# Layer 1's gate product: three 256-column matmuls a step in place of 512 and 256 columns, with no copy and addition of two halves

## Chip, cores, metric

The kernel runs on one core of a Trainium2 chip. The metric is device time in microseconds of one execution; the time before is the median of 3 runs. The core's engines are named as in the profile: PE (TensorE's matmuls), PEld (its weight loads), DVE (VectorE), ACT (ScalarE), POOL (GpSimd) and SP (SyncE, which here issues DMA transfers). SBUF is the core's working memory, and PSUM the eight accumulation banks into which PE writes.

## What is computed

Two layers of a diffusion transformer on 256 tokens of width 2048 and 256 context tokens, in fp32. Layer 0 mixes with a Fourier transform, layer 1 with attention. Only layer 1 matters here: 64 query heads of 64 channels, 8 key and value heads, a window of 128 tokens beside the context, and a sink in the softmax. Its result is multiplied by a gate, silu(z), before the output product:

```python
q, k, v, z = jnp.split(h @ w_in, [D_BRANCH, D_BRANCH + kvw, D_BRANCH + 2 * kvw], axis=-1)
...
y = jnp.moveaxis(o, 0, 1).reshape(b, n, D_BRANCH) * jax.nn.silu(z)
...
x = x + gate * (y @ w_out[i])
```

The change touches the product that makes z: 256 tokens by 2048, times 2048 by 4096.

## The kernel before

**Two parts for each number.** Products of full precision are made of a high part, which PE reads as fp32r, and a low part, the remainder. `split` makes them: ACT casts the high part (line 66), DVE subtracts it to get the low part (line 67). For a weight W = wh + wl and an activation h = hi + lo, the product is wh·hi + wh·lo + wl·hi. The helper `mm3` (lines 145 to 147) issues these as three matmuls into one PSUM region. The activations of layer 1 lie in 16 tiles `hx1[k]` of 128 x 512, one for each 128 input channels: columns 0 to 255 are the high parts of the 256 tokens, columns 256 to 511 the low parts. Both parts are therefore side by side.

**A gate block** is 128 of the 4096 gate channels, and there are 32. A block takes 16 steps, one for each `k`, in two units of 8 steps. Each step has the weights as the stationary operand (128 x 128, wh or wl) and the activations as the moving one. Before, wh meets all 512 columns of `hx1[k]` in one matmul (line 1451), so that wh·hi comes to stand in columns 0 to 255 of the PSUM bank and wh·lo in columns 256 to 511; wl meets the 256 high columns in a second matmul (line 1453), added to columns 0 to 255. In the last step the order of the two is turned round. Then ACT copies the second half out of PSUM into a tile `zs` (line 1457), DVE adds the first half to it (line 1458), ACT takes the tanh of half of that (line 1459), and DVE makes (tanh + 1)·z (line 1460), which is twice silu(z). The product with the attention's output is line 1472.

**Around it.** The blocks are fillers for PE in the attention of layer 1. A loop over 64 heads `i` puts down the scores of head `i` (`stage_s`), a unit of other work, the values of head `i - 2` (`stage_o`), and another unit. The units come from a list: the query product of a group of 8 heads (8 units), then that group's 4 gate blocks (2 units each), and at the end the first part of the output product.

- `stage_s`: scores on PE (lines 1489 and 1490), mask and maximum on DVE (line 1491), exponential on ACT (line 1494), normalised probabilities f as a high part on ACT (line 1506) and a low part on DVE (line 1507), then a DMA transpose `ft<-f` (line 1509).
- `stage_o`: values times transposed probabilities on PE (lines 1524 and 1525), out through ACT (line 1530) and DVE (line 1531).
- Queries: out of PSUM on ACT (line 1357), rotated on POOL (lines 1132 to 1138), transposed on PE (line 1370) and split (lines 1373 to 1376).
- Weights: loaded by SP 1 MB at a time into three buffers `raw` (line 50), split in halves, one unit ahead of use.

The order on each engine isn't the order of the code: a scheduler sets it when the program is built, by its own estimate of when each instruction could run. An engine runs its instructions in that order, and waits at the head of its list.

Of the kernel before, what the change touches and what calls it, by code (L numbers as in the profile page):

```python
# [10 lines left out]
F32 = mybir.dt.float32  # L11
# [3 lines left out]
ALU = mybir.AluOpType  # L15
AX = mybir.AxisListType

P = 128
D = 2048
KT = D // P  # L20
DB = 4096
NB = DB // P
N = 256
# [9 lines left out]
def tile_dit(ctx: ExitStack, tc: tile.TileContext, a: dict, out: bass.AP):  # L33
    nc = tc.nc
    V, S, PE, GP = nc.vector, nc.scalar, nc.tensor, nc.gpsimd
# [8 lines left out]
    def psum():  # L44
        return pp.tile([P, 512], F32, tag="ps", name="ps")
# [98 lines left out]
    def mm3(o, wh, wl, xh, xl, start, stop):  # L144
        PE.matmul(o, wh, xh, start=start, stop=False)  # L145
        PE.matmul(o, wh, xl, start=False, stop=False)  # L146
        return PE.matmul(o, wl, xh, start=False, stop=stop).ins  # L147
# [711 lines left out]
    with tc.tile_pool(name="yp", reuse_waits="tile", bufs=32) as ypool:  # L859
# [39 lines left out]
        if True:  # L899
# [21 lines left out]
            for kg in range(4):  # L921
# [10 lines left out]
                for j in range(4):  # L932
                    k = kg * 4 + j
                    wh, wl = w[j // 2]
                    for b in range(4):
                        q = slice((j % 2) * 512 + b * P, (j % 2) * 512 + (b + 1) * P)
# [7 lines left out]
            for b in range(4, NB):  # L944
# [9 lines left out]
                o = psum()  # L954
                for k in range(KT):
# [13 lines left out]
                    wh, wl = w[k // 8]  # L969
                    q = slice((k % 8) * P, (k % 8 + 1) * P)  # L970
# [60 lines left out]
        for i in range(32):  # L1031
            sw, kg = i // 16, i % 16
            if kg == 0:
                o = [psum() for _ in range(8)]
# [9 lines left out]
            if kg == 14:  # L1044
                q = gt0[:, sw * 8 : sw * 8 + 8].rearrange("p k s -> p (k s)")
# [21 lines left out]
            for j, b in [(j, b) for b in range(8) for j in range(2)] if edge else [(j, b) for j in range(2) for b in range(8)]:  # L1067
                q = slice(b * P, (b + 1) * P)
# [35 lines left out]
    with tc.issue_after(st_end[0]):  # L1104
        o = psum()
# [34 lines left out]
    with tc.tile_pool(name="h1", reuse_waits="tile", bufs=16) as h1p:  # L1140
        hx1 = []
# [3 lines left out]
        with tc.tile_pool(name="kvp", reuse_waits="tile", bufs=2) as kvp:  # L1145
# [4 lines left out]
            for k in range(KT):  # L1150
                z2 = kvp.tile([P, 1024], F16, tag="hz", name="hz", bufs=16)
                t = kvp.tile([P, 512], F32, tag="ht", name="ht")
                for s in range(2):
                    q = slice(s * N, (s + 1) * N)
# [40 lines left out]
            o = [[psum() for _ in range(2)] for _ in range(4)]  # L1195
            for kg in range(8):
# [16 lines left out]
                for j in range(2):  # L1213
                    k = kg * 2 + j
                    wh, wl = w[j]
                    for tb in range(4):
                        c = tb // 2 * 512 + tb % 2 * P
                        for kv in range(2):
                            q = slice(kv * 512, (kv + 1) * 512)
# [40 lines left out]
        with tc.tile_pool(name="at", reuse_waits="tile", bufs=2) as at:  # L1260
# [55 lines left out]
            def o1_step(k, os_, wh, wl):  # L1316
                while len(yh) <= min(k + 4, NB - 1) and (len(yh) < 28 or fin):
                    y_split(len(yh))
                for tb in range(2):
                    mm3(os_[tb], yh[k][:, tb * P : (tb + 1) * P], yh[k][:, N + tb * P : N + (tb + 1) * P], wh, wl, k == 0, k == NB - 1)  # L1320
# [17 lines left out]
            def prep_kk(hk):  # L1338
                kkh = at.tile([P, 512], F32R, tag="kkh", name="kkh")
                kkl = at.tile([P, 512], F32R, tag="kkl", name="kkl")  # L1340
                b = (hk % 2) * 64
                src = kT[hk // 2][b : b + 64, :]
                for c in (0, 64):
                    S.copy(kkh[c : c + 64, :], src)
                for c in (0, 64):
                    GP.tensor_tensor(kkl[c : c + 64, :], src, kkh[b : b + 64, :].bitcast(F32), op=ALU.subtract)
                kk[hk] = (kkh, kkl)

            def finish_q(hk, oq):
                qr = []  # L1350
                for tb in range(2):
                    t = act()
                    if hk == 0:
                        roped(t, oq[tb], tb, actp, "act")
                    else:
                        t0 = act()
                        S.copy(t0, oq[tb])
                        roped(t, t0, tb, actp, "act", GP)
                    qr.append(t)
                if hk:  # L1360
                    prep_kk(hk)
                for p2 in range(2):
                    defer.append((slot[0], lambda p2=p2: q_turn(hk, p2, qr)))
# [38 lines left out]
            def prep(u):  # L1402
                kind, n, i, _ = u
                if kind == "o":
                    return w1_next()
                src = (kind, n, i // 2)
                if src not in raws1:
                    raws1[src] = raw(a["wq"][n, i // 2] if kind == "q" else a["wz1"][n])
                return half_split(raws1[src], i % 2)
# [3 lines left out]
            def emit_unit():  # L1413
                if pos[0] >= len(ulist):
                    return
                u = ulist[pos[0]]
                if pos[0] not in ready:
                    ready[pos[0]] = prep(u)
                if pos[0] + 1 < len(ulist):
                    ready[pos[0] + 1] = prep(ulist[pos[0] + 1])  # L1420
                w = ready.pop(pos[0])
                pos[0] += 1
                kind, n, i, o = u
                if kind == "o":
                    if n == 0:
                        oA.extend([psum(), psum()])
                    for j in range(2):
                        o1_step(n * 2 + j, oA, *(t[:, j * 512 : (j + 1) * 512] for t in w))
                    return
                wh, wl = w  # L1430
                if kind == "q":
                    if i == 0:
                        o += [psum(), psum()]
                    if (n, i) == (0, 4):
                        with tc.issue_after(last_cast[0]):
                            prep_kk(0)
                    for j in range(2):
                        k = i * 2 + j
                        q = slice(j * 512, (j + 1) * 512)
                        for tb in range(2):  # L1440
                            mm3(o[tb], hx1[k][:, tb * P : (tb + 1) * P], hx1[k][:, N + tb * P : N + (tb + 1) * P], wh[:, q], wl[:, q], k == 0, k == KT - 1)
                    if i == 7:
                        finish_q(n, o)
                else:
                    if i == 0:
                        o.append(psum())
                    for k in range(i * 8, i * 8 + 8):
                        q = slice((k % 8) * P, (k % 8 + 1) * P)
                        for part in (0, 1) if k < KT - 1 else (1, 0):
                            if part == 0:  # L1450
                                PE.matmul(o[0], wh[:, q], hx1[k], start=k == 0, stop=k == KT - 1)  # L1451
                            else:
                                PE.matmul(o[0][:, 0:N], wl[:, q], hx1[k][:, 0:N], start=False, stop=False)  # L1453
                    if i == 1:
                        th = at.tile([P, N], F32, tag="th", name="th", bufs=3)
                        zs = at.tile([P, N], F32, tag="zs", name="zs", bufs=1)
                        S.copy(zs, o[0][:, N : 2 * N])
                        V.tensor_tensor(zs, o[0][:, 0:N], zs, op=ALU.add)
                        S.activation(th, zs, AF.Tanh, scale=0.5)
                        V.scalar_tensor_tensor(th, th, 1.0, zs, op0=ALU.add, op1=ALU.mult)  # L1460
                        szs[n] = th
                        emit_y(n)
# [3 lines left out]
            def emit_y(blk):  # L1466
                if blk not in szs or (blk, 1) not in obs or blk in ydone:
                    return
                ydone.add(blk)
                if blk % 2 == 0:  # L1470
                    y1.append(act())
                V.scalar_tensor_tensor(y1[blk // 2][:, (blk % 2) * N : (blk % 2 + 1) * N], obs[blk, 1], dsc[:, blk // 4 : blk // 4 + 1], szs.pop(blk), op0=ALU.mult, op1=ALU.mult)
                if blk % 2:
                    ypairs.append(slot[0] // 2)
# [62 lines left out]
            for i in range(first):  # L1537
                emit_unit()
                if i == 2:
                    for hp in range(4):  # L1540
                        k_turn(hp)
                if i == 5:
                    for half in range(2):
                        d_turn(half)
                if i >= 8 and defer:
                    defer.pop(0)[1]()

            def filler():
                j = slot[0]
                slot[0] += 1  # L1550
                emit_unit()
                if defer and defer[0][0] + 2 < j:
                    defer.pop(0)[1]()
# [23 lines left out]
        with tc.tile_pool(name="fin", reuse_waits="tile", bufs=1) as fp:  # L1577
# [41 lines left out]
            o = [[psum() for _ in range(2)] for _ in range(2)]  # L1619
            for kg in range(16):  # L1620
# [10 lines left out]
                for j in range(2):  # L1631
                    k = kg * 2 + j
                    wh, wl = w[j]
                    for tb in range(2):
                        for c in range(2):
                            q = slice(c * 512, (c + 1) * 512)
# [4 lines left out]
            o = [psum() for _ in range(2)]  # L1641
# [70 lines left out]
            for h in range(2):  # L1712
                q = slice(h * 256, h * 256 + 256)
# [107 lines left out]
```

## Time and profile before

| | before |
|---|---|
| median of 3 runs | 1764.61 us (1764.34 to 1765.5) |
| profiled execution | 1766.34 us |
| its span, first to last instruction | 1764.5 us |
| PE busy | 1728.8 us, 9539 matmuls |
| DVE busy | 1421.9 us |
| ACT busy | 1148.4 us |
| the gate blocks run from about | 1142 us to 1575 us |
| granted TensorE clock over the span | 0.998 |

The table's busy times are of one profiled execution; the median is of runs without a profile. A matmul's duration in the profile reaches from its start to the modelled end of its results, so consecutive matmuls overlap, and the pace of PE is read from the distance between starts. In a row such as `ps<-h,wh 128*128 128x512` the names are output, moving and stationary operand, then the size of the weights and that of the result.

### The profile page before, as it was taken

How to read it: one execution, taken by the hardware profiler on the slowest of the kernel's cores; microseconds unless marked ns; L12 is line 12 of the kernel's file. 1: busy time of each engine (PE TensorE's matmuls, PEld its weight loads, DVE VectorE, ACT ScalarE, POOL GpSimd, SP SyncE). 2: the span in 40 equal slices, each digit the busy share in tenths (PEclk: the TensorE clock that was granted, in tenths of full speed). 3: DMA queues.
4: the chain of work that ended last, by engine and by line, in shares of the span. 5: the costliest groups of instructions: out<-in, count | busy, mean ns of one | idle time of the engine just before them, and what ended most of it. 6: DMA issues, size and time to landing. Idle time of an engine off the chain costs nothing.

```text
span 1764.5 us, 26891 instructions
## 1 busy us (share of the span) xinstructions
PE 1728.8 (98%) x9539; PEld 1149.6 (65%) x9539; DVE 1421.9 (81%) x2475; ACT 1148.4 (65%) x2197; POOL 361.3 (20%) x485
## 2 busy tenths in 40 slices
PE   6999999999999999999999999999999999999998
PEld 4679999644444444446444745788888878877464
DVE  5769888798676787777698686899899889998755
ACT  5545556476777755465235596688888788897643
POOL 0002111211222105212311111412303221251001
PEclk9999999999999999999999999999999999999999
DMA  9998999778998869977996594688997897888643
GB/s 394 417 342 254 275 273 257 295 282 303 340 314 299 312 227 378 372 254 258 394 341 229 181 362 155 191 198 198 222 212 200 204 212 207 210 192 283 225 172 120
DMA packets 232296, 465.66 MB, mean 264 GB/s; under 512 B 154497, under 2 KB 154897, under 8 KB 205281
## 3 DMA queue, kind: packets, MB, share of 16 engines
q1 hardware_dynamic: 180672, 331.41, 58.5%
q0 software_dynamic: 47344, 125.58, 22.2%
q10 hardware_dynamic: 4144, 6.95, 1.2%
q8 instruction: 75, 1.23, 0.3%
q14 instruction: 61, 0.49, 0.1%
HBM read 419.30 MB, written 12.59 MB: 245 GB/s over the span
## 4 chain that ended last, share of the span: by engine, by line
PE 80%; DVE 8%; DMA 7%; ACT 3%; issue 2%; POOL 0%; POOLq 0%; ACTq 0%; DVEq 0%; SPq 0%
PE ps L145 23%; PE ps L146 23%; PE ps L147 22%; PE ps L1451 3%; DMA ft<-f 3%; DMA raw<-in_awp 2%; PE ps L1453 2%; DVE wl L67 2%; DVE f L1507 1%; PE ps L286 1%; DVE ps L1491 1%; PE ps L1489 1%; PE ps L1490 1%; PE ps L1524 1%; PE ps L1525 1%
## 5 line engine op out<-in xcount | busy, mean ns | idle before, releaser
L67 DVE TENSOR_TENSOR wl<-raw,wh 128x1024 fp32r<-128x1024 f32 x152 | 203.1, 1337 | 38.4 <-ACT wh L66 27.2
L146 PE MATMUL ps<-act,wf 128*128 128x512 f16 x512 | 194.0, 379 | 0.0
L147 PE MATMUL ps<-act,wf 128*128 128x512 f16 x512 | 191.1, 379 | 0.0
L145 PE MATMUL ps<-act,wf 128*128 128x512 f16 x512 | 189.8, 379 | 0.6 <-ACT wf L137 0.3
L66 ACT CAST wh<-raw 128x1024 fp32r<-128x1024 f32 x152 | 158.2, 1042 | 48.0 <-PE ps L146 29.1
L1451 PE MATMUL ps<-h,wh 128*128 128x512 f32 x512 | 184.8, 397 | 0.0
L145 PE MATMUL ps<-y,wf 128*128 128x512 f16 x448 | 169.8, 379 | 0.8 <-ACT wf L137 0.8
L146 PE MATMUL ps<-y,wf 128*128 128x512 f16 x448 | 169.8, 379 | 0.0
L147 PEld LDWEIGHTS <-wf 128*128 128x128 f16 x960 | 93.9, 98 | 113.3
L145 PEld LDWEIGHTS <-wf 128*128 128x128 f16 x960 | 93.7, 98 | 113.2 <-ACT wf L137 4.2
L147 PE MATMUL ps<-y,wf 128*128 128x512 f16 x448 | 164.9, 379 | 0.0
L146 PEld LDWEIGHTS <-wf 128*128 128x128 f16 x960 | 93.9, 98 | 109.0
L137 ACT ACTIVATE wf<-raw,nrm 128x1024 f16<-128x1024 f32 x56 | 63.5, 1145 | 130.1 <-PE ps L147 78.6
L1453 PE MATMUL ps<-h,wl 128*128 128x256 f32 x512 | 138.7, 281 | 0.3 <-DVE wl L67 0.3
L138 DVE SCALAR_TENSOR_TENSOR wf<-raw,tn,wf 128x1024 f16<-128x1024 f32 x64 | 79.8, 1281 | 42.5 <-ACT wf L137 41.8
L1494 ACT ACTIVATE p<-ps,mx 128x512 f32<-128x512 f32 x128 | 88.1, 689 | 39.7 <-DVE mx L1491 36.6
L829 ACT ACTIVATE act<-act 128x512 f32<-128x512 f32 x178 | 109.4, 616 | 5.9 <-DMA act<-in_wo 4.5
L790 POOL DMA_DIRECT2D wa<-in_adw x64 | 34.2, 535 | 371.7 <-PE ps L147 144.9
L1507 DVE SCALAR_TENSOR_TENSOR f<-p,sm,f 128x512 f16<-128x512 f32 x128 | 103.5, 829 | 8.3 <-ACT f L1506 8.0
L1451 PEld LDWEIGHTS ps<-h,wh 128*128 128x128 f32 x512 | 96.2, 188 | 18.9
L1506 ACT ACTIVATE f<-p,sm 128x512 f16<-128x512 f32 x128 | 88.0, 717 | 31.1 <-DMA ft<-f 18.4
L146 PE MATMUL ps<-wl,h 128*128 128x512 f32 x256 | 101.8, 398 | 0.6 <-DVE wl L67 0.6
(430 smaller groups left out, 4863.6 us busy)
## 6 DMA issues: line engine op xcount, KB each, us to landing
raw<-in_wz SPq DMA_DIRECT2D x64, 1024.0 KB, 5.9
raw<-in_awp SPq DMA_DIRECT2D x32, 1024.0 KB, 12.7
zr<-in_adw SPq DMA_DIRECT2D x64, 512.0 KB, 7.0
wa<-in_adw POOLq DMA_DIRECT2D x64, 512.0 KB, 6.6
act<-in_wo POOLq DMA_DIRECT2D x128, 256.0 KB, 7.7
raw<-in_wo SPq DMA_DIRECT2D x32, 1024.0 KB, 8.2
raw<-in_wq SPq DMA_DIRECT2D x32, 1024.0 KB, 5.3
raw<-in_wu SPq DMA_DIRECT2D x32, 1016.0 KB, 6.7
```

Source lines behind the costliest of these rows:

```text
L66: last_cast[0] = S.copy(h, src).ins
L67: last_sub[0] = eng.tensor_tensor(l, src, h.bitcast(F32), op=ALU.subtract).ins
L138: last_sub[0] = V.scalar_tensor_tensor(w[:, 1], src, up, w[:, 0], op0=ALU.mult, op1=ALU.subtract).ins
L145: PE.matmul(o, wh, xh, start=start, stop=False)
L146: PE.matmul(o, wh, xl, start=False, stop=False)
L147: return PE.matmul(o, wl, xh, start=False, stop=stop).ins
L829: S.activation(t, t, AF.Square, accum_out=c)
L1451: PE.matmul(o[0], wh[:, q], hx1[k], start=k == 0, stop=k == KT - 1)
L1453: PE.matmul(o[0][:, 0:N], wl[:, q], hx1[k][:, 0:N], start=False, stop=False)
L1494: S.activation(pt[tb], so[tb], AF.Exp, bias=mx[:, tb : tb + 1], scale=-1.0, accum_out=sm[:, tb : tb + 1])
L1506: fa = S.activation(f[:, 0:512], pt[tb], AF.Copy, scale=sm[:, tb : tb + 1]).ins
L1507: f_last[:] = fa, V.scalar_tensor_tensor(f[:, 512:1024], pt[tb], sm[:, tb : tb + 1], f[:, 0:512], op0=ALU.mult, op1=ALU.subtract).ins
```

## The change

Every step of a gate block goes through `mm3` with the moving operand cut into its two halves: wh with the 256 high columns, wh with the 256 low columns, wl with the high columns, all three added into columns 0 to 255 of the bank. The sum is complete in PSUM when the last step ends. The copy and the addition go, the tile `zs` with them, and tanh and the last operation read the bank.

```diff
                     for k in range(i * 8, i * 8 + 8):
                         q = slice((k % 8) * P, (k % 8 + 1) * P)
-                        for part in (0, 1) if k < KT - 1 else (1, 0):
-                            if part == 0:
-                                PE.matmul(o[0], wh[:, q], hx1[k], start=k == 0, stop=k == KT - 1)
-                            else:
-                                PE.matmul(o[0][:, 0:N], wl[:, q], hx1[k][:, 0:N], start=False, stop=False)
+                        mm3(o[0][:, 0:N], wh[:, q], wl[:, q], hx1[k][:, 0:N], hx1[k][:, N : 2 * N], k == 0, k == KT - 1)
                     if i == 1:
                         th = at.tile([P, N], F32, tag="th", name="th", bufs=3)
-                        zs = at.tile([P, N], F32, tag="zs", name="zs", bufs=1)
-                        S.copy(zs, o[0][:, N : 2 * N])
-                        V.tensor_tensor(zs, o[0][:, 0:N], zs, op=ALU.add)
+                        zs = o[0][:, 0:N]
                         S.activation(th, zs, AF.Tanh, scale=0.5)
                         V.scalar_tensor_tensor(th, th, 1.0, zs, op0=ALU.add, op1=ALU.mult)
```

Six lines fewer stand in the file, so what was line 1459 and later has a number lower by 6 in the changed kernel: tanh is line 1453 there, the high part of f 1500, the first values matmul 1518. The new matmuls carry the helper's lines, 145 to 147.

On PE, the start of the first gate block, whose first two steps are shown; `h` with a number is the tile `hx1[k]`. Before:

```order
L1451 MATMUL ps<-h_10253,wh 128x512
L1453 MATMUL ps<-h_10253,wl 128x256
L1451 MATMUL ps<-h_10258,wh 128x512
L1453 MATMUL ps<-h_10258,wl 128x256
L1451 MATMUL ps<-h_10263,wh 128x512
```

After:

```order
L145 MATMUL ps<-h_10253,wh 128x256
L146 MATMUL ps<-h_10253,wh 128x256
L147 MATMUL ps<-h_10253,wl 128x256
L145 MATMUL ps<-h_10258,wh 128x256
L146 MATMUL ps<-h_10258,wh 128x256
L147 MATMUL ps<-h_10258,wl 128x256
```

A step has three matmuls, and two in a row have the weights wh.

On ACT, the instructions behind the copy of the second gate block; `qa` and `qb` are split queries, `p` the exponentials, `es` the sink's share, `th` the gate's tanh. Before:

```order
L1373 CAST qa<-ps 64x512
L1374 CAST qb<-ps 64x512
L1459 ACTIVATE th<-zs 128x256
L1494 ACTIVATE p,sm<-ps,mx 128x512
L1495 ACTIVATE es<-mx,sink 128x2
L1506 ACTIVATE f<-p,sm 128x512 x2
L66 CAST wh<-raw 128x1024
L1373 CAST qa<-ps 64x512
L1374 CAST qb<-ps 64x512
```

After, at the same place:

```order
L1373 CAST qa<-ps 64x512
L1374 CAST qb<-ps 64x512
L1488 ACTIVATE p,sm<-ps,mx 128x512
L1489 ACTIVATE es<-mx,sink 128x2
L66 CAST wh<-raw 128x1024
L1373 CAST qa<-ps 64x512
L1374 CAST qb<-ps 64x512
L1500 ACTIVATE f<-p,sm 128x512 x2
```

The tanh has left this place (it stands where the copy stood), and the two f have moved behind a weight cast and the second pair of query copies. There are such exchanges on ACT and DVE throughout the stretch, most of them by a place or two; SP's list of weight loads and transposes changes in its first part.

## The prediction

> **What bounds the kernel now.** I read the page first, then the busy time of the stretch that the change touches, then what PE waited for there, and last the matmuls of one gate block in order of time.
>
> ```profile
> span 1764.5 us, 26891 instructions
> PE 1728.8 (98%) x9539; PEld 1149.6 (65%) x9539; DVE 1421.9 (81%) x2475; ACT 1148.4 (65%) x2197; POOL 361.3 (20%) x485
> ```
>
> PE is busy 98% of the span, and PE and PEld have the same number of instructions, so each matmul brings a weight load of its own, also where two in a row use the same weights. The profiled execution took 1766.34 us, 1.84 us more than its span, and lies 1.7 us above the median of the runs, 1764.61 us. The differences worked out below are added to the median.
>
> ```profile
> core 0: us, PE busy (x) PEld busy (x) DVE busy (x) ACT busy (x) POOL busy (x), PEclk, DMA share, GB/s
> 1142.00:1575.00 433.00, 429.37 (x2366) 356.69 (x2365) 401.79 (x746) 358.98 (x724) 105.23 (x78) 1.00 0.87 208
> ```
>
> This is the stretch in which all 32 gate blocks run, woven into the attention. PE is busy 429.4 of 433.0 us at the full clock (1.00), but VectorE is at 401.8 / 433.0 = 93% and the DMA engines at 0.87. Three resources are close to their limit; PE is the first. What PE waited for, in the same stretch:
>
> ```profile
> PE ps L1524 <- DMA ft<-f: 2.1, 4, 1.2
> PE ps L146 <- DVE wl L67: 0.6, 2, 0.4
> PE ps L1370 <- POOL act L1138: 0.5, 1, 0.5
> PE ps L1453 <- DVE wl L67: 0.3, 1, 0.3
> ```
>
> In all 3.5 us, of which 0.9 us ended with VectorE's low weight half and 2.1 us with a DMA transpose of the probabilities. So the stage runs at PE's pace, and two things count: what a step costs on PE, and how much of these 3.5 us goes or is added.
>
> **PE's pace, the main term.** A step was one matmul of 512 columns (weights wh, line 1451) and one of 256 (weights wl, line 1453), 512 times. It becomes three of 256: wh on the high half, wh again on the low half, wl on the high half. The columns streamed are the same, 768; there is one matmul and one weight load more.
>
> ```profile
> L1451 PE MATMUL ps<-h,wh 128*128 128x512 f32 x512 | 184.8, 397 | 0.0
> L1453 PE MATMUL ps<-h,wl 128*128 128x256 f32 x512 | 138.7, 281 | 0.3 <-DVE wl L67 0.3
> L1453 PEld LDWEIGHTS ps<-h,wl 128*128 128x128 f32 x512 | 96.6, 189 | 3.5 <-DVE wl L67 0.7
> L1451 PEld LDWEIGHTS ps<-h,wh 128*128 128x128 f32 x512 | 96.2, 188 | 18.9
> ```
>
> These durations (397 and 281 ns, loads 188 and 189) overlap each other, so they can't be added; the price is the distance from one start to the next. In the second gate block, in order of time:
>
> ```profile
> 1150.05 0.40 PE L1451 MATMUL ps<-h,wh 128*128 128x512 f32 x1
> 1150.29 0.28 PE L1453 MATMUL ps<-h,wl 128*128 128x256 f32 x1
> 1150.40 0.39 PE L1451 MATMUL ps<-h,wh 128*128 128x512 f32 x1
> ...
> 1154.91 0.39 PE L1451 MATMUL ps<-h,wh 128*128 128x512 f32 x1
> 1155.14 0.40 PE L1453 MATMUL ps<-h,wl 128*128 128x256 f32 x2
> 1155.38 0.40 PE L1451 MATMUL ps<-h,wh 128*128 128x512 f32 x1
> ```
>
> From the first to the fifteenth wh matmul there are 14 steps in 1154.91 - 1150.05 = 4.86 us: 347.1 ns a step. The row with x2 is the block's end, where two 256-column matmuls with new weights each follow one another: together they last 0.40 us where one lasts 0.28, so the second began 0.12 us after the first; with the group's mean of 281 ns for one, about 118 ns. That is the pace which the new step would have, inside this very stage: 3 x 118 = 354 ns. The change costs 354 - 347.1 = 6.9 ns a step, 512 x 6.9 = 3.5 us.
>
> Two other stages bound the 118 ns, the nearest rows with three 256-column matmuls a step:
>
> ```profile
> 31.42 0.28 PE L146 MATMUL ps<-dl,xh 128*128 128x256 f32 x1
> ...
> 34.59 0.28 PE L147 MATMUL ps<-dh,xl 128*128 128x256 f32 x1
> 222.85 0.28 PE L145 MATMUL ps<-act,wmh 128*127 128x256 f32 x1
> ...
> 228.48 0.28 PE L147 MATMUL ps<-act,wml 128*127 128x256 f32 x1
> ```
>
> The first run is 28 matmul starts in 3.17 us, 113.2 ns each; the second 47 in 5.63 us, 119.8 ns each, with the same weights (wmh) twice in a row as the new step has them. By the first a step takes 339.6 ns and the change wins 512 x 7.5 = 3.8 us; by the second it takes 359.4 and costs 512 x 12.3 = 6.3 us. I take 118, because it was measured among the same tiles, in the same stage, and lies nearer to the second.
>
> Of this the Trainium skill has a rule (TensorE: Matmul & The Clock Gate, "Back-to-back issue gap"): a warm matmul starts N/2.4 + 2.5 ns after the one before. By it the old step is 215.8 + 109.2 = 325.0 ns, the new one 327.5, and the change costs an estimated 1.3 us instead of 3.5. The step of 347.1 ns in the trace is longer than that rule allows, so the rows decide.
>
> **What leaves ACT and DVE.** Behind each block the copy (line 1457) and the addition (line 1458) go; the tanh and the last operation now read the PSUM bank itself.
>
> ```profile
> L1472 DVE SCALAR_TENSOR_TENSOR act<-ob,dsc,th 128x256 f32<-128x256 f32 x28 | 13.9, 495 | 0.1
> L1460 DVE SCALAR_TENSOR_TENSOR th<-th,zs 128x256 f32<-128x256 f32 x31 | 13.5, 436 | 0.4
> L1459 ACT ACTIVATE th<-zs 128x256 f32<-128x256 f32 x31 | 12.9, 416 | 3.3 <-DVE zs L1458 3.2
> L1458 DVE TENSOR_TENSOR zs<-ps,zs 128x256 f32<-128x256 f32 x31 | 12.7, 411 | 0.0
> L1457 ACT COPY zs<-ps 128x256 f32<-128x256 f32 x32 | 11.9, 373 | 0.7
> ```
>
> That is 32 x 0.411 = 13.2 us of DVE and 32 x 0.373 = 11.9 us of ACT. The tanh out of PSUM isn't in the trace: between the copy out of PSUM, 373 ns, and its own 416. The last operation with one operand in PSUM lies between 411 ns (line 1458, the same mix) and 495 (line 1472); I take 411, so nearly no change. At most 32 x 0.059 = 1.9 us of DVE are given back. DVE goes from 93% to about (401.8 - 13.2) / 436.5 = 89%. None of it is PE's time: it is worth only what it takes from PE's 3.5 us of waits. The bank is released by the second operation behind the block, as before. I count half of the 0.9 us that ended with DVE, 0.45 us, since the addition was one of many operations that a late wl stood behind, and nothing of the rest.
>
> **Sum.** 3.5 - 0.45 = +3.05 us: 1764.61 + 3.05 = 1767.7 us; the profiled execution would come to 1769.4. That is 0.17%, just under 0.2% (3.5 us), which is about what a measurement of this kernel can tell from no change.
>
> **Rivals.**
>
> *The relief pays for the pace* (17%). If the lighter DVE and ACT let every f and wl come early, all 3.5 us of waits go and the sum is 3.5 - 3.5 = 0: 1764.6. For it: DVE at 93%. Against it: the longest wait is on the transpose's own DMA.
>
> *The new order makes PE wait for transposes* (20%), the rival that ends slower. The scheduler placed ACT's and DVE's instructions anew. Behind the second gate block the normalised probabilities f (line 1506) now stand behind one weight cast and two q copies:
>
> ```profile
> L66 ACT CAST wh<-raw 128x1024 fp32r<-128x1024 f32 x112 | 116.5, 1040 | 0.8 <-PE ps L1453 0.4 <-PE ps L1451 0.3
> L1374 ACT CAST qb<-ps 64x512 fp32r<-64x512 f32 x14 | 8.2, 583 | 0.2
> L1373 ACT CAST qa<-ps 64x512 fp32r<-64x512 f32 x14 | 8.0, 575 | 0.0
> ```
>
> So f may begin 1.04 + 0.58 + 0.58 = 2.2 us later there, its transpose with it. Transposes leave little room: their landing varies by more than that, and PE already waits for some.
>
> ```profile
> DMA to landing us min/median/max: 3.0/5.1/7.8
> 1502.57 0.28 PE L1524 MATMUL ps<-ft,v 128*128 128x256 f16 x1 [0.41 <-DMA ft<-f]
> ```
>
> It decides from the point at which a transpose lands after PE has finished the matmuls placed ahead of line 1524. Priced at the stage's waits doubled, 3.5 us more: 3.5 + 3.5 = +7.0, 1771.6. Against it: PE's own order between scores and values hardly moves, and the relief works the other way.
>
> *The short pace* (7%). If the new steps run at 113.2 ns a matmul, the sum is -3.8 - 0.45 = -4.25: 1760.4. Against it: all 256-column matmuls of this stage start at 118.
>
> *The added weight load isn't hidden* (1%). Then each step pays the load's 188 ns, 512 x 0.188 = 96 us: 1861. Against it stands the old step: its two loads alone last 377 ns, more than the 347.1 ns of the whole step, so loads do run beside matmuls. In the Trainium skill (the same page, "The mechanism" in Part 3) stands that a weight load overlaps a running matmul only where the row groups differ, and these weights fill all rows; by that rule the load would be exposed. The trace disagrees with it here.
>
> That the change doesn't do what it says can be excluded: PE's list holds three matmuls a step, and the copy and the addition are gone.
>
> **Chances.** The forecast keeps 55%: its own range is the pace at 117 to 119 ns (351 to 357 ns a step, +2.0 to +5.1) less 0 to 0.9 us of relief, so +1.1 to +5.1, 1765.7 to 1769.7, of which I put four parts in ten above 3.5 us. Slower by over 0.2%: 0.22 + 0.20 + 0.01 = 0.43. Faster: the short pace, 0.07, and 0.03 of the relief case, 0.10. Within 0.2%: 0.33 + 0.14 = 0.47. The range from 1763.0 to 1772.0 leaves out the short pace (7%), the exposed load (1%), 2% of the relief case and two fifths of the new waits (8%): 18%.
>
> **What would show it.** In the profile after, steps of line 145 to 147 at 354 ns from wh to wh show the main term right; 340 or 359 would show one of the bounds. The share of DVE in the stage should fall to about 89%. PE's waits in the stage, on DMA ft and on wl, should come to about 3 us: near 0 is the relief case, 6 or more the order's. Wrong altogether would be a span that moves by more than the steps and these waits together, or the copy and addition showing up as PE time.

## The result and the profile after

The changed kernel is faster: 1761.26 us against 1764.37 us in the median of 12 runs each, a ratio of 0.9979 with a 95% interval of 0.9972 to 0.9986. That is 3.1 us, 0.2%, where the prediction had 3 us more. The profiled execution took 1761.24 us. Its page and the stretch of the gate blocks:

```profile
span 1759.3 us, 27829 instructions
PE 1726.3 (98%) x10051; PEld 1173.5 (67%) x10051; DVE 1404.7 (80%) x2443; ACT 1141.0 (65%) x2165; POOL 355.5 (20%) x485
1142.00:1575.00 433.00, 431.66 (x2888) 383.60 (x2887) 389.01 (x722) 356.63 (x702) 105.35 (x83) 1.00 0.84 207
```

PE has 512 matmuls and 512 weight loads more, DVE and ACT 32 instructions fewer each. DVE's busy share of the stretch fell from 93% to 389.0 / 433.0 = 90%, near the 89% that was forecast, and PE's rose from 429.4 to 431.7 us. The spans differ by 5.2 us, more than the medians; 1.7 us of that lie ahead of the first scores (at 1128.73 us before, 1127.05 us after), where the order on the engines is the same in both.

PE's pace, in the changed kernel's second gate block and in a unit near the end, the first matmul of a step each time:

```profile
1148.55 0.28 PE L145 MATMUL ps<-h,wh 128*128 128x256 f32 x1
...
1153.85 0.28 PE L145 MATMUL ps<-h,wh 128*128 128x256 f32 x1
...
1541.87 0.28 PE L145 MATMUL ps<-h,wh 128*128 128x256 f32 x1
...
1544.32 0.28 PE L145 MATMUL ps<-h,wh 128*128 128x256 f32 x1
```

The first two rows are 15 steps apart: 5.30 us, 353.3 ns a step, as forecast. The last two are 7 steps apart: 2.45 us, 350.0 ns. Over all blocks the steps lie at 350.8 ns in the mean, against 347.7 before; left out are steps with other matmuls or a wait between them, and some 30 in either kernel that take about 90 ns longer. So the pace costs 3.1 ns a step, 1.6 us in all, not 3.5.

PE's waits from the first scores on. First the kernel before, then the changed one (in all, times, longest, in us):

```profile
PE ps L1524 <- DMA ft<-f: 4.1, 5, 2.0
PE ps L146 <- DVE wl L67: 1.4, 3, 0.8
PE ps L1524 <- DVE ft L1517: 0.8, 1, 0.8
PE ps L1370 <- POOL act L1138: 0.5, 1, 0.5
PE ps L1453 <- DVE wl L67: 0.3, 1, 0.3
```

```profile
PE ps L1518 <- DMA ft<-f: 2.6, 2, 2.0
PE ps L1518 <- ACT wh L66: 1.3, 1, 1.3
```

Eleven waits with 7.1 us of idle time became three with 3.9 us. The two that both kernels share come at the stage's start, of 2.0 us at about 1140 and 1.2 to 1.3 us at about 1165. Every later wait went, and one of 0.5 us at 1592 is new.

An idle wait is shorter than what it costs. Before, in order of time:

```profile
1537.58 0.40 PE L1451 MATMUL ps<-h,wh 128*128 128x512 f32 x1
1538.28 0.39 PE L1453 MATMUL ps<-h,wl 128*128 128x256 f32 x1 [0.30 <-DVE wl L67]
```

The starts are 0.70 us apart where 0.23 is usual, so 0.47 us were lost, and only 0.30 are shown as idle: a matmul's duration runs on for about 0.16 us after the next could have begun, and hides that much of each wait (0.155 to 0.166 us in all fourteen waits of the two lists). Eight waits fewer are 3.2 us of idle time and some 8 x 0.16 = 1.3 us beneath it. With 1.6 us for the pace the sum is -3.2 - 1.3 + 1.6 = -2.9 us, where the medians differ by 3.1. From the first scores to the end the two traces differ by 3.5 us; the last 0.6 us of that stay open.

Where DVE makes a transpose late can be seen in head 48, whose transposed probabilities are the ones that PE waited for at 1502.57 before. Its last scores matmul and DVE's mask on it (line 1491, 1485 after), before and then after:

```profile
1484.02 0.39 PE L1490 MATMUL ps<-kkl,qa 128*128 128x512 f32 x1
1490.22 0.75 DVE L1491 CUSTOM_DVE_ANT_0 ps<-ps,mask,nsink 128x512 f32<-128x512 f32 x1
```

```profile
1481.43 0.39 PE L1484 MATMUL ps<-kkl,qa 128*128 128x512 f32 x1
1484.36 0.75 DVE L1485 CUSTOM_DVE_ANT_0 ps<-ps,mask,nsink 128x512 f32<-128x512 f32 x1
```

The scores lay finished for 5.8 us before, and for 2.5 us after, until DVE came to them. Over heads 4 to 60 the mean of this delay is 3.8 us before, of which DVE stood idle for 0.2, and 1.6 us after. The rest of the way from scores to landed transposes differs far less: from issue to landing it takes 4.9 us before and 4.7 after. So the transposes land 3.6 us ahead of the values product in the mean, where they landed 1.5 us ahead.

### The profile page after: what moved, and what is told of

It is laid out like the page before. It is cut to its first block, busy times and chain, and to the rows that moved or that the text cites. A ratio compares the mean times of both kernels' runs of the same rounds, so it can differ in the third digit from the quotient of the medians.

```text
span 1759.3 us, 27829 instructions
## 1 busy us (share of the span) xinstructions
PE 1726.3 (98%) x10051; PEld 1173.5 (67%) x10051; DVE 1404.7 (80%) x2443; ACT 1141.0 (65%) x2165; POOL 355.5 (20%) x485
## 4 chain that ended last, share of the span: by engine, by line
PE 91%; DVE 3%; DMA 3%; ACT 2%; issue 1%; POOL 0%; ACTq 0%; POOLq 0%; SPq 0%; DVEq 0%
PE ps L145 27%; PE ps L146 27%; PE ps L147 27%; DMA raw<-in_awp 2%; PE ps L1518 2%; PE ps L1483 2%; PE ps L1484 2%; PE ps L1519 2%; PE ps L286 1%; ACT wf L137 1%; DMA ft<-f 0%; ACT act L877 0%; PE ps L1370 0%; DVE wf L138 0%; DVE act L984 0%
## 5 line engine op out<-in xcount | busy, mean ns | idle before, releaser
L147 PEld LDWEIGHTS <-wf 128*128 128x128 f16 x960 | 93.9, 98 | 113.2
L145 PE MATMUL ps<-h,wh 128*128 128x256 f32 x512 | 145.5, 284 | 0.0
L147 PE MATMUL ps<-h,wl 128*128 128x256 f32 x512 | 142.9, 279 | 0.0
L146 PE MATMUL ps<-h,wh 128*128 128x256 f32 x512 | 142.9, 279 | 0.0
```

## Experiments

Two theories were weighed, and each has rivals in the expectations. **Load**: DVE, the fullest queue beside PE, and perhaps ACT, makes PE wait, and 13 us less work on it removes the waits. **Hop**: it isn't the amount of work, but the tanh at the head of ACT's list that waits for DVE's addition. The scheduler's order changes in every kernel, so chance of the order stands beside both. Each kernel was timed in five rounds beside the kernel before. The waits in the table at the end are idle times of PE after 1170 us, past the stage's start. They are of one profiled execution, which can lie off the median: that of `pace_alone` took 1763.11 us, 2.8 us less than its median, and that of `load_in_place` 1766.85 us, 2.2 us more.

### The pace alone, and the lighter queues alone

`pace_alone` has the three matmuls, with the second in its own half of the bank, and keeps copy and addition:

```diff
-                        for part in (0, 1) if k < KT - 1 else (1, 0):
...
+                        PE.matmul(o[0][:, 0:N], wh[:, q], hx1[k][:, 0:N], start=k == 0, stop=False)
+                        PE.matmul(o[0][:, N : 2 * N], wh[:, q], hx1[k][:, N : 2 * N], start=False, stop=False)
+                        PE.matmul(o[0][:, 0:N], wl[:, q], hx1[k][:, 0:N], start=False, stop=k == KT - 1)
```

> Three 256-column matmuls a step, the second into columns 256 to 511, with the copy and the addition kept. Theory (the lighter ACT and DVE took PE's waits away, the pace costs 1.65 us): PE's matmuls of a step at 351 ns, PE's waits about as before (12 of them, 7.2 us idle from 1127 us on), +1 to +2 us against before. Rival (the new order of the scheduler, not the load, took the waits away): the order changes here too, so the waits can go to 4 us, and the time is -3 to +2. Rival (256-column matmuls are the gain): faster than before by 2 us or more with the waits unchanged.

Measured 1765.91 us, ratio 1.0010 (1.0001 to 1.0019): slower by about 1.7 us. Steps at 350.9 ns. The pace costs time; it isn't the gain. The waits were not as expected: the trace has seven with 5.2 us in all, against eleven before (the expectation counted twelve), though the copy and the addition are there. So part of the waits goes with the order, or with the one execution that was traced.

`relief_alone` has the old matmuls without copy and addition:

```diff
-                        zs = at.tile([P, N], F32, tag="zs", name="zs", bufs=1)
-                        S.copy(zs, o[0][:, N : 2 * N])
-                        V.tensor_tensor(zs, o[0][:, 0:N], zs, op=ALU.add)
+                        zs = o[0][:, 0:N]
```

> Matmuls of 512 and 256 columns as before, the copy and the addition left out, so the product of wh with the low parts is left out of z. Theory (lighter ACT and DVE): PE's waits fall from 12 to about 3 (3.9 us idle), step at 347 ns, -4.0 to -5.5 us against before, 1 to 2 us less than the changed kernel. Rival (chance of the order): waits anywhere between 2 and 9 us, no fixed relation to the changed kernel. Rival (pace is the gain): as before.

Measured 1759.70 us, ratio 0.9974 (0.9963 to 0.9984): 4.6 us faster. Steps at 347.7 ns. The parts add up: +1.7 and -4.6 make -2.9, where both together measured -3.1.

### Which of the two instructions

`no_add` keeps the copy and drops the addition; `no_copy` the other way round:

```diff
-                        V.tensor_tensor(zs, o[0][:, 0:N], zs, op=ALU.add)
-                        S.activation(th, zs, AF.Tanh, scale=0.5)
+                        S.activation(th, o[0][:, 0:N], AF.Tanh, scale=0.5)
```

```diff
-                        S.copy(zs, o[0][:, N : 2 * N])
-                        V.tensor_tensor(zs, o[0][:, 0:N], zs, op=ALU.add)
+                        V.tensor_tensor(zs, o[0][:, 0:N], hx1[0][:, 0:N].bitcast(F32), op=ALU.add)
```

> Matmuls as before, the copy on ACT kept, the addition on DVE left out (tanh reads the first half, the last operation the copy, so z is not the sum). Theory with DVE as the queue that makes PE wait: -3 to -5 us, PE's waits about 4 us idle. With ACT as that queue: -1 to 0.

> Matmuls as before, the copy on ACT left out, the addition on DVE kept with an SBUF tile that is always ready as its second operand (so z is not the sum). Theory with DVE as the queue that makes PE wait: -1 to 0 us. With ACT, or the hop from ACT to DVE at the head of DVE's list, as the cause: -3 to -5.

`no_add` measured 1759.56 us, ratio 0.9974 (0.9965 to 0.9983): all of the gain. `no_copy` measured 1768.11 us, ratio 1.0019 (1.0010 to 1.0028): slower than before, though ACT has 12 us less to do. Its waits of PE, after 1170 us:

```profile
PE ps L1523 <- DMA ft<-f: 4.8, 4, 2.4
PE ps L146 <- DVE wl L67: 0.2, 1, 0.2
PE ps L1370 <- POOL act L1138: 0.2, 1, 0.2
```

So it is the addition on DVE that counts, not the copy. But neither theory forecast a loss for `no_copy`, and in its trace the tanh waits for DVE far more than before:

```profile
ACT th L1458 <- DVE zs L1457: 14.1, 13, 2.4
```

That made the hop a serious rival: the kernels so far with the addition ahead of the tanh had the waits, and those without it hadn't.

### Three runs that loaded the wrong place, and one that moved work to POOL

To tell load from hop, a copy and an addition of the same size were put back into the changed kernel, behind the gate, on SBUF tiles that nobody waits for: both (`load_back`), the addition alone (`add_back`), the copy alone (`copy_back`).

```diff
                         V.scalar_tensor_tensor(th, th, 1.0, zs, op0=ALU.add, op1=ALU.mult)
+                        jk = at.tile([P, N], F32, tag="jk", name="jk", bufs=1)
+                        S.copy(jk, hx1[0][:, 0:N].bitcast(F32))
+                        V.tensor_tensor(jk, hx1[1][:, 0:N].bitcast(F32), jk, op=ALU.add)
```

> The changed kernel, with a copy on ACT and an addition on DVE of the same size put back behind each block, on SBUF tiles that nothing else waits for. Theory (DVE's and ACT's load makes PE wait): PE's waits come back to 5 to 7 us idle, as with the pace alone, +1 to +2 us against before. Rival (the shorter way from a block's last matmul to its gate, or the freed bank, is what helps): -2.5 to -3.5 us as the changed kernel. Rival (the scheduler's order by chance): anywhere from -4 to +4.

> The changed kernel with only an addition on DVE put back, on SBUF tiles. Theory with DVE as the cause: 0 to +2 us against before. With ACT as the cause: -2 to -3.5. Chance of the order: no relation to which engine is loaded.

> The changed kernel with only a copy on ACT put back, on SBUF tiles. Theory with DVE as the cause: -2 to -3.5 us against before, as the changed kernel. With ACT as the cause: 0 to +2.

Measured: `load_back` 1765.22 us, ratio 1.0004 (0.9994 to 1.0013); `add_back` 1772.29 us, 1.0044 (1.0030 to 1.0058); `copy_back` 1761.79 us, 0.9988 (0.9979 to 0.9996). The first and the last look like the load theory's numbers, the second is worse than any theory had it, and none is a test. The tile `jk` of `add_back`:

```profile
L1456 DVE TENSOR_TENSOR jk<-h,h x32: 411/422/1503, 1092.1 to 1148.5; 128x256 f32<-128x256 f32 x32
```

All 32 additions ran between 1092 and 1149 us: their operands were ready, so the scheduler pulled them ahead of the blocks. All copies of `copy_back` ran before 1126 us, and the pairs of `load_back` before 1188 us. There they held up the first heads, and `add_back`'s PE waits are nearly all of that place:

```profile
PE ps L1520 <- DMA ft<-f: 9.1, 3, 7.3
```

Its trace is 10.7 us longer than the changed kernel's: 5.2 of it lie in the wait of 7.3 us, which is of 2.0 us there, and 4.4 ahead of the first scores. After 1188 us nothing was loaded in any of the three.

`pool_y` left the old gate as it was, and took 28 x 0.495 us from DVE, the product with the attention, by making it on POOL:

```diff
...
+                if blk < 28:
+                    GP.tensor_tensor(yd, obs[blk, 1], szs.pop(blk), op=ALU.mult)
+                    GP.tensor_scalar(yd, yd, dsc[:, blk // 4 : blk // 4 + 1], None, op0=ALU.mult)
+                else:
+                    V.scalar_tensor_tensor(yd, obs[blk, 1], dsc[:, blk // 4 : blk // 4 + 1], szs.pop(blk), op0=ALU.mult, op1=ALU.mult)
```

> The kernel before, with the product of gate and attention (line 1472) taken from DVE for 28 of 32 blocks and made on POOL in two operations; the gate's matmuls, copy and addition stay. Theory (DVE's load): 28 x 0.495 = 13.9 us less on DVE, PE's waits fall to about 4 us idle, -3 to -5 us against before, and less time than the changed kernel, since the step stays at 347 ns. Rival (something in the gate's own copy and addition): 0. Rival (POOL becomes late with the rotated queries): slower, with waits on POOL.

Measured 1770.66 us, ratio 1.0039 (1.0026 to 1.0051). DVE had 430.3 us from first to last scores instead of 437.1, only 7 us less where 13.9 had been counted: the low parts of f alone (line 1512 here) took 866 ns each instead of 829, 4.8 us in all. A new wait arose on ACT:

```profile
ACT act L1284 <- POOL act L1475: 8.7, 5, 1.9
```

ACT's sums of squares now wait 8.7 us for POOL's product, at the head of the list that also casts the weights. DVE came to the scores no earlier than before, after 4.1 us in the mean, and PE's waits after 1170 us are 7.8 us. So this run settles nothing between the theories; the work taken from DVE brought no gain here, and that ACT's wait is the reason wasn't tested.

### Load against hop, each alone

Four kernels put the two apart. `load_in_place` is the changed kernel with the copy and the addition on the gate tile itself, so that they can't run early; `load_nohop` is the same on the old matmuls.

```diff
                         V.scalar_tensor_tensor(th, th, 1.0, zs, op0=ALU.add, op1=ALU.mult)
+                        jk = at.tile([P, N], F32, tag="jk", name="jk", bufs=1)
+                        S.copy(jk, th)
+                        V.tensor_tensor(jk, th, jk, op=ALU.add)
```

`hop_only` (old matmuls) and `hop3` (new ones) have no copy and no addition, but the tanh waits for DVE. The part that both share:

```diff
-                        S.activation(th, zs, AF.Tanh, scale=0.5)
+                        bz = at.tile([P, 1], F32, tag="bz", name="bz", bufs=2)
+                        V.tensor_scalar(bz, o[0][:, 0:1], 0.0, None, op0=ALU.mult)
+                        S.activation(th, zs, AF.Tanh, bias=bz, scale=0.5)
```

> The changed kernel, with a copy on ACT and an addition on DVE put back behind each block's gate, on the gate tile itself, so that they can't run before the block (in the three runs before, the added work was pulled ahead of the stage). Theory 1 (DVE's and ACT's load makes PE wait): PE's waits after the first 45 us of the stage come back to 2 to 5 us idle, the time to -1 to +2 us against before. Theory 2 (ACT's tanh waiting for DVE's addition at the head of ACT's list is the cause): waits after the stage's start stay under 1 us, -2 to -3.5 us against before.

> Matmuls of 512 and 256 columns, no copy and addition ahead of the tanh (the product of wh with the low parts is left out of z), a copy and an addition of the same size behind the gate. Theory 1 (load): as before, -1 to +1 us, waits after the stage's start about 3 to 5 us idle. Theory 2 (tanh waiting for DVE): -3.5 to -5 us, waits after the stage's start about 1 us.

> Matmuls of 512 and 256 columns, no copy and addition (the product of wh with the low parts is left out of z), but a DVE instruction on one column ahead of each tanh, for which the tanh waits. Theory 1 (load): DVE is about 10 us lighter than before, -3 to -5 us. Theory 2 (tanh waiting for DVE): waits after the stage's start come back to 3 to 5 us, -1 to +1 us against before.

> The changed kernel with a DVE instruction on one column ahead of each tanh, for which the tanh waits. Theory 1 (load): -2 to -3.5 us against before, near the changed kernel. Theory 2 (tanh waiting for DVE): 0 to +2 us against before.

| kernel | us | ratio (95%) | tanh waits for DVE | DVE busy, first to last scores | scores wait for DVE, mean | PE's waits after 1170 us |
|---|---|---|---|---|---|---|
| before | 1764.37 | 1 | yes | 437.1 | 3.8 | 3.9 |
| load_nohop | 1769.35 | 1.0030 (1.0020 to 1.0041) | no | 435.2 | 3.7 | 5.4 |
| no_copy | 1768.11 | 1.0019 (1.0010 to 1.0028) | yes | 432.8 | 3.5 | 5.2 |
| hop_only | 1760.28 | 0.9977 (0.9969 to 0.9986) | yes | 421.4 | 2.7 | 0.4 |
| relief_alone | 1759.70 | 0.9974 (0.9963 to 0.9984) | no | 421.3 | 2.9 | 1.4 |
| no_add | 1759.56 | 0.9974 (0.9965 to 0.9983) | no | 424.2 | 2.2 | 1.2 |
| *three matmuls a step:* | | | | | | |
| pace_alone | 1765.91 | 1.0010 (1.0001 to 1.0019) | yes | 436.1 | 3.2 | 2.3 |
| load_in_place | 1764.68 | 1.0003 (0.9994 to 1.0012) | no | 432.6 | 3.6 | 2.2 |
| hop3 | 1760.45 | 0.9978 (0.9970 to 0.9987) | yes | 423.4 | 1.4 | 0 |
| changed | 1761.26 | 0.9979 (0.9972 to 0.9986) | no | 421.7 | 1.6 | 0.5 |

The hop falls: with it and without the load (`hop_only`, `hop3`) the time is as good as without both. The load stays: with it and without the hop the gain is gone, in both pairs. `load_nohop` even lost 5.3 us, where the load theory had -1 to +1. In these two kernels the addition also needs ACT's copy, as it did before; `no_copy`, whose addition needs nothing of ACT, lost as well, so the loss doesn't need that wait. The waits' rows, `load_in_place` first, then `load_nohop`, then `hop_only`; `hop3` has none:

```profile
PE ps L146 <- DVE wl L67: 1.8, 3, 0.9
PE ps L147 <- DVE wl L67: 0.4, 1, 0.4
```

```profile
PE ps L1525 <- DMA ft<-f: 3.5, 4, 2.1
PE ps L146 <- DVE wl L67: 0.8, 2, 0.5
PE ps L1525 <- ACT jk L1460: 0.7, 1, 0.7
PE ps L1525 <- ACT f L1507: 0.4, 1, 0.4
```

```profile
PE ps L1524 <- DMA ft<-f: 0.4, 2, 0.2
```

The table's fifth column is DVE's busy time in the view of stages, from each kernel's own first scores to its last; here are the rows of before, of `no_copy`, of `no_add` and of the changed kernel, with PE, PEld, DVE, ACT and POOL in that order:

```profile
1128.73:1598.82 470.09, 463.65 (x2530) 383.44 (x2529) 437.06 (x812) 391.09 (x792) 123.29 (x94) 1.00 0.85 206
```

```profile
1126.81:1600.70 473.89, 466.39 (x2530) 384.85 (x2529) 432.80 (x814) 385.00 (x762) 128.11 (x94) 0.99 0.84 204
```

```profile
1126.87:1592.33 465.46, 462.17 (x2530) 383.72 (x2529) 424.15 (x780) 391.58 (x792) 120.57 (x94) 1.00 0.85 208
```

```profile
1127.05:1594.41 467.36, 463.43 (x3042) 408.88 (x3041) 421.65 (x783) 384.99 (x763) 117.64 (x94) 1.00 0.83 208
```

Five kernels with 421 to 424 us on DVE have 0 to 1.4 us of late waits; five with 433 to 437 us have 2.2 to 5.4. The sixth column, from the end of a head's last scores matmul to the start of DVE's mask on it (mean of heads 4 to 60), shows the way: 1.4 to 2.9 us in the lighter five and 3.2 to 3.8 us in the heavier. ACT doesn't sort them: `no_add` has 391.6 us and `no_copy` 385.0. `pool_y` doesn't fit by busy time (430.3 us, 7.8 us of late waits), but its scores wait for DVE as in the heavier five. Within those the waits don't follow the load. The scheduler's order is the likely reason: the three heavy kernels with the old matmuls spread from 0 to +5.3 us against before, as much as the effect itself, the three light ones from -4.6 to -4.1. How much of the waits of before is its particular order can't be told from these runs, since no run held the order fixed while the load changed.

No kernel that makes the whole gate was measured clearly faster than the changed one; the ratio of `hop3`, 0.9978, lies within its interval.

## Why the prediction was wrong

**PE as the bound, the full clock, the second most loaded engine:** right. **The pace:** the mechanism was right and the size was off, 1.6 us instead of 3.5. The 118 ns of a 256-column matmul were read inside the old steps; in a row of three the mean is 350.8 / 3 = 116.9 ns. The bound rows (113 and 120) held it. The rule of the Trainium skill that the prediction names (TensorE: Matmul & The Clock Gate, "Back-to-back issue gap"), by which the term was an estimated 1.3 us, came nearer to the difference of 1.6 us, though not to the steps.

**The relief** is the step that failed: "I count half of the 0.9 us that ended with DVE, 0.45 us ... and nothing of the rest". Measured are 3.2 us of idle time and some 1.3 us under it, and 4.6 us in `relief_alone`. Three readings went wrong there. The waits were taken by what ended last, so those on the transpose were left to the DMA. But a transpose starts when f is made, and f needs DVE's mask on the scores. In the three late waits on transposes of the trace before (at 1434, 1503 and 1549 us) the scores had lain finished for 5.1 to 5.8 us until DVE came to them; the mean after is 1.6. So those waits go with DVE's queue as well. The idle time was taken for the loss, though each wait costs about 0.16 us more than it shows. And the list stopped at 1575 us, where the gate blocks end; two waits of 0.8 us each came after it, at 1584 on wl and at 1622 on the transposed f, and neither is there in the changed kernel. What the prediction took for the operations themselves came out: the last one takes 415 ns out of PSUM (411 was assumed), the tanh 385 ns.

**The rival "the relief pays for the pace"** was the right mechanism, given 17%, and was priced at zero from the same two wrong sizes, 3.5 us of pace and 3.5 us of waits; with the measured ones it is -2.9. **The order** as a rival: f was moved behind a cast and two query copies at the second block as read. It is the f of head 4, and was finished 1.3 us later after its scores than before; its transposes still landed 2.6 us ahead of the values product (2.8 before), so the move cost nothing at its place. The rival wasn't empty, though: `load_nohop` and `no_copy` show waits on transposes of up to 2.4 us. **The short pace** didn't come (116.9 ns, not 113.2). **The exposed weight load** didn't either: 512 more loads of 188 ns came with 1.6 us more.

The share of DVE, named as a sign, came near the forecast (90% against 89%). PE's waits in the stage, forecast at about 3 us and near zero in the relief case, are 1.3 us, all at the stage's start.

## To carry to other kernels

In this kernel a second engine was 93% busy under a bound engine at 99%, and small waits of the bound engine belonged to it even where a DMA was named as what ended them: ask which queue stood ahead of that DMA, and how long finished work lay there. An instruction that is taken from that queue can be worth more than what the bound engine's pace loses for it (here 4.6 us against 1.7). When work is added to test a queue, tie it to data that is made in the stage, or the scheduler may do it elsewhere, as it did in three runs here.

## What was not expected of the hardware

Three fp32 matmuls of 256 columns with a weight load each run at 350.8 ns a step, 1% above one of 512 and one of 256 (347.7), though they load 128 x 128 fp32 weights once more. And each wait of PE in these two traces shows about 0.16 us less idle time than it takes, since the matmul before it is still recorded as busy.
